# The end of an attention layer put in a written order: sums and norms on four engines, and GpSimd's weight scaling tied to VectorE

## The chip, the cores and the metric

One core of a Trainium2 chip runs the whole program in one launch. The metric is device time in microseconds (us), the median of the runs; lower is better. Five engines matter: TensorE (PE) multiplies, VectorE (DVE) and ScalarE (ACT) work on elements and read the products out of PSUM, GpSimd (POOL) works on elements in SBUF, and SyncE (SP) issues the DMA transfers. Each works through its own list of instructions in order, and semaphores tie the lists together.

## The reference

A decoder trunk for one sequence of 512 tokens of width 1024 in float32: a pooling layer, then a stick-breaking attention layer with 16 heads of 64, each followed by a squared-ReLU MLP of width 4096, all with a norm before and after. The part around the change is this:

```python
# attention layer (layer 1); k, v were projected from the stream after layer 0
h = rms_norm(x, mix_pre_g[layer])
q = jnp.matmul(h, w_q[j]).reshape(B, S, N_HEADS, HEAD_DIM).transpose(0, 2, 1, 3)
o = stick_breaking_attention(q, k, v)
m = jnp.matmul(o.transpose(0, 2, 1, 3).reshape(B, S, HD), w_o[j])
x = x + rms_norm(m, mix_post_g[layer])
h = rms_norm(x, mlp_pre_g[layer])          # then the MLP on h
...
def rms_norm(x, g):
    y = xf * lax.rsqrt(jnp.mean(xf * xf, axis=-1, keepdims=True) + EPS)
    return (y * g.astype(jnp.float32)).astype(x.dtype)
```

The gains of the norms before the k, q and v projections are applied to the rows of the weights.

## The kernel before, in words

Tokens are held in four tiles of 128 (`t` = 0 to 3), the width in eight chunks of 128. Products of full precision are made of three fast ones (`mm3`): each operand is split into a high part (a cast to fp32r, on ScalarE) and a low part (operand minus high part, on VectorE).

**Weights split ahead of their use.** Weights that are needed late are loaded, scaled if a norm's gain belongs to them, split, and stored to DRAM (`kept`) while VectorE and ScalarE have time; when they are needed, both parts are loaded from there. During attention `split_here` and `low_here` do this one tile at a time. Each tile in `going` carries a stage. A step `W` calls `split_here`, which stores tiles whose low part is made, scales, casts the high part (`nc.scalar.copy`, L211, into one of three buffers, `xn3[:, len(here) % 3]`), and loads the next tile; it then calls `fill`, which asks for the next weight. A step `w` calls `low_here` (L227, VectorE). The tiles in order are: v6 in two halves, q4, k4, q5, k5, o0, o1, q6, k6, q7, k7, o2 to o7, and the MLP's up0 to up3. The k and q tiles of this list are scaled on GpSimd (`wide_gains`, L166), v6 on ScalarE (`gains`, L157).

**The order of attention.** `ATT_ORDER` is a list written by hand, and PE, ACT, DVE and POOL follow it exactly (`tc.manual_schedule`). The letters: `J`/`Q` project keys/queries of a pair of heads, `j`/`q` read them out of PSUM (casts L1103, L1104, L1116 on ScalarE, low parts `kl` L1106 and L1118 on VectorE), `S` scores (L1145), `G` sigmoids (L1169, L1173), `X` the scan (L1178), `M` the multiplication of its result (L1270), `T` transposes (L1194) with copies on ScalarE (L1196), `A` the product with v (L1204), `a` its split (`mixed_out`, L372 and L373), `V`/`v`/`F` the value projection, its sums and its operands, `O`/`o` products of the output projection for the first pairs and their sums (`out_sum`, L1234). The digits are the pair and the head or token tile. SP is not written out; the compiler's own scheduler places its transfers.

**The end.** After the list `contract` multiplies the last four chunks (pairs 4 to 7) with their weights for tile after tile (L410 to L412), adds them to `y[t]` (L518), and runs an `Update` for each tile: squares (L376, ScalarE), the gain (L445, GpSimd for one half, VectorE for the other), the factor (`rstd`, L380 and L389), the sum into the stream `x` (L457, VectorE) with squares of it, the second factor, the norm (L474), and the transpose of the normed tile (L483) with its split into `xnh`, `xnl`. Here only PE's order is written; the scheduler orders the other engines and may also move these instructions up among those of the list. The transposes of tiles 2 and 3 follow in the MLP, between its first products (L773 to L775).

Of the kernel before, what the change touches and what calls it, by code (L numbers as in the profile page):

```python
# [10 lines left out]
F32 = mybir.dt.float32  # L11
F32R = mybir.dt.float32r
ACT = mybir.ActivationFunctionType
ALU = mybir.AluOpType
# [39 lines left out]

ATT_ORDER = [
    (w[0], int(w[1:2] or 0), int(w[2:] or 0))
    for w in """V5 W N2 v5 V0 N3 W V3 F3 v0 J0 v3 F2 W j0 w Q0 q0 F1 W w V1 V2 v1 W w v2 S0 G0 X00 M00 J1 X01 V4 M01 j1
    T00 T01 F4 v4 Q1 q1 W w V6 W v6 w
    S1 G1 X10 M10 X11 Q2 M11 q2 W w J2 A0 W j2 w a0 T10 T11
    S2 G2 X20 M20 X21 Q3 M21 q3 W w J3 A1 W j3 w a1 T20 T21  # L60
    S3 G3 X30 M30 X31 Q4 M31 q4 W w J4 A2 W j4 w a2 T30 T31
    S4 G4 X40 M40 X41 Q5 M41 q5 W w J5 A3 W j5 w a3 O00 W w O01 o00 T40 o01 T41 O02 W w O03 o02 o03
    S5 G5 X50 M50 X51 Q6 M51 q6 W w J6 A4 W j6 w a4 T50 T51
    S6 G6 X60 M60 X61 Q7 M61 q7 W w J7 A5 W j7 w a5 T60 T61
    S7 G7 X70 M70 X71 W w O10 M71 O11 W w A6 o10 a6 o11 O12 W w T70 O13 T71 o12 W A7 o13 a7""".split()
]


# [16 lines left out]
def trunk(ctx, tc, x, consts, gcol, grow, pw, wup, wdn, wq, wk, wv, wo, out):  # L85
# [35 lines left out]
    def spare_tile():  # L121
        return work.tile([P, D], F32, tag="spare", name=name("spare"))
# [38 lines left out]
    def wide_gains(lo, n):  # L161

        def scaled(raw):
            c = raw.rearrange("p (k c) -> p k c", k=n)
            g = gc[:, lo : lo + n].unsqueeze(2).broadcast_to((P, n, D // n))
            nc.gpsimd.tensor_tensor(out=c, in0=c, in1=g, op=ALU.mult)  # L166

        return scaled
# [32 lines left out]
    def split_here():  # L201
        for x in [x for x in going if x[1] == 4]:
            going.remove(x)
            keep_parts(x[0], x[3], x[2])
        for x in going:
            k, m, raw, hi, scaled = x
            if m == 1 and scaled is not None:
                scaled(raw)
            elif m == 2:
                hi = x[3] = xn3[:, len(here) % 3].bitcast(F32R)  # L210
                nc.scalar.copy(hi, raw)  # L211
            x[1] += 1
        if here:
            k, src, scaled = here.pop(0)
            n = len(here) % 4
            if n < 2:
                raw = wts.tile([P, D], F32, tag="raw", bufs=2, name=name("raw"))
            else:
                raw = spare_tile() if n == 2 else work.tile([P, D], F32, tag="grow", name=name("apart"))
            with tc.issue_after(latest["sp"].ins):  # L220
                nc.sync.dma_start(raw, src)
            going.append([k, 1, raw, None, scaled])

    def low_here():
        x = next(x for x in going if x[1] == 3)
        _, _, raw, hi, _ = x
        nc.vector.tensor_tensor(out=raw, in0=raw, in1=hi.bitcast(F32), op=ALU.subtract)  # L227
        x[1] = 4
# [146 lines left out]
    def square_sum(src, junk, st, col):  # L375
        latest["act"] = nc.scalar.activation(junk, src, ACT.Square, scale=D**-0.5, accum_out=st[:, col : col + 1])  # L376
# [9 lines left out]
    def rstd(st, col, total=None):  # L386
        total = both_sums(st, col) if total is None else total
        r = st[:, col + 3 : col + 4]
        latest["pool"] = nc.gpsimd.tensor_tensor(out=r, in0=total, in1=mhalf, op=ALU.pow)  # L389
        return r  # L390
# [31 lines left out]
    class Update:  # L422
# [24 lines left out]
        def product(self, n):  # L447
            return self.beside if n and self.cuts is not NS else self.scaled

        def add(self, between=None):  # L450
            r = rstd(self.st, 0, self.total)
            if between is not None:
                with tc.issue_after(latest["dve"].ins):
                    between()
            x = xt[self.t]
            for n, cut in enumerate(self.sums):
                latest["dve"] = nc.vector.scalar_tensor_tensor(  # L457
                    out=x[:, cut], in0=self.product(n)[:, cut], scalar=r, in1=x[:, cut], op0=ALU.mult, op1=ALU.add,
                )
                if self.final:  # L460
                    nc.sync.dma_start(out[TS[self.t], cut], x[:, cut])
                else:
                    square_sum(x[:, cut], self.xn[:, cut], self.st, 4 + n)

        def rstd(self):
            self.r = rstd(self.st, 4)
# [527 lines left out]
    with tc.tile_pool(name="att", bufs=1, reuse_waits="tile") as ap:  # L994
# [244 lines left out]
        with tc.manual_schedule(engines={on.PE, on.Activation, on.DVE, on.Pool}):  # L1239
            for what, i, a in ATT_ORDER:  # L1240
                if what == "V":
                    value_product(i)
                elif what == "v":
                    value_out(i)
                elif what == "F":
                    form(i)
                elif what == "W":
                    split_here()
                    fill()
                elif what == "w":  # L1250
                    low_here()
                elif what == "N":
                    need(i)
                elif what in "JQ":
                    project(("k" if what == "J" else "q", i))
                    fill()
                elif what == "j":
                    keys(i)
                elif what == "q":
                    queries(i)  # L1260
                elif what == "S":
                    pzs[i] = scores((qs[i], ks[i]))
                elif what == "G":
                    for a in range(2):
                        ws[i, a] = sigmoids(pzs[i], a)
                elif what == "X":
                    es[i, a] = scanned(a)
                elif what == "M":
                    w = ws[i, a]
                    latest["dve"] = nc.vector.tensor_tensor(out=w, in0=w, in1=es.pop((i, a)), op=ALU.mult)  # L1270
                elif what == "T":
                    parts[i, a] = transposed(ws.pop((i, a)))
                elif what == "A":
                    mix_pair(i)
                elif what == "a":
                    mixed_out(i)
                elif what == "O":
                    out_product(i, a)
                    if a == T - 1:
                        fill()  # L1280
                elif what == "o":
                    out_sum(i, a)
        assert not here and not going, (here, going)
        with tc.issue_after(latest["sp"].ins):
            gpost1, gpre1 = gain_row(R_MIX_POST1), gain_row(R_MLP_PRE1, spare_tile())
        wos[2] = [get(("o", 4 + c)) for c in range(4)]
        behind.update(latest)
        fill(2)
        with tc.manual_schedule(engines={on.PE}):
            contract([os[4 + c] for c in range(4)], wos[2], y, False, lambda t, y: Update(t, gpost1, y, gpre=gpre1),  # L1290
                     range(T), True)


    with tc.tile_pool(name="mlp1", bufs=1, reuse_waits="tile") as mp:
# [64 lines left out]
```

## Time and profile before

| | |
|---|---|
| time, median of 3 runs | 921.25 us (920.29 to 921.39) |
| profiled execution | 918.29 us, span 916.5 us |
| mean granted clock of TensorE | 0.991 |
| PE busy | 893.8 us, 98% |
| DVE, ACT, POOL busy | 713.4, 548.3, 107.9 us |
| DMA | 185.06 MB |
| attention's scores, pairs 0 to 7, begin at | 389 to 536 us of the span |
| output projection's end and its norms | about 558 to 604 us |

A row of the timeline gives the start and the length in us, the engine, the line, the operation, output and inputs, shape and count, and in brackets the idle time before it and what ended that. A row of the list of waits gives who waited, for whom, the sum in us, how often, and the longest. A row of stretches gives the bounds, the length, busy time and count for PE, weight loads, DVE, ACT and POOL, then the granted clock, the DMA share and GB/s. Rows of groups end in count, busy time, mean ns of one, and the idle time before with its releasers.

### The profile page before, as it was taken

What the parts mean: (1) busy time and instruction counts of PE and PEld (TensorE: products, weight loads), DVE (VectorE), ACT (ScalarE), POOL (GpSimd) and SP (SyncE); (2) the same over time, 40 slices, a digit from 0 to 9 for tenths busy, and PEclk for the clock granted to TensorE, in tenths of its full rate; (3) what the DMA queues carried; (4) which work ended last, traced back from release to release, by engine and by line L of the source; (5) the groups of instructions that cost most, each with busy time, mean ns of one, the idle gap of its engine ahead of it and who ended that gap; (6) DMA issues with size and microseconds to landing.
All of it is one profiled execution on the core that took longest, in us unless ns stands there. A gap on an engine that the chain in (4) does not pass through costs nothing.

```text
span 916.5 us, 11949 instructions
## 1 busy us (share of the span) xinstructions
PE 893.8 (98%) x4522; PEld 774.3 (84%) x4522; DVE 713.4 (78%) x718; ACT 548.3 (60%) x890; POOL 107.9 (12%) x94
## 2 busy tenths in 40 slices
PE   9999999999999999999999999799999999999996
PEld 7998888888888888878778877698888888888886
DVE  5966798987979876798885885765596875967956
ACT  6667756575996656557767862456554454454632
POOL 2100000000000023021210000302040300403103
PEclk9999999999999999999999999899999999999999
DMA  7443557287695904999778988232504233043102
GB/s 284 167 181 138 184 207 262 106 296 273 238 374 195 329 38 177 352 413 417 272 283 301 400 302 342 105 144 97 200 32 143 109 135 118 29 156 114 44 27 92
DMA packets 51247, 185.06 MB, mean 202 GB/s; under 512 B 5312, under 2 KB 5786, under 8 KB 51190
## 3 DMA queue, kind: packets, MB, share of 16 engines
q1 hardware_dynamic: 51042, 184.28, 54.5%
q8 instruction: 36, 0.59, 0.3%
q14 instruction: 21, 0.17, 0.1%
q10 hardware_dynamic: 148, 0.02, 0.0%
HBM read 138.14 MB, written 46.14 MB: 201 GB/s over the span
## 4 chain that ended last, share of the span: by engine, by line
PE 84%; DVE 6%; ACT 3%; DMA 3%; issue 2%; POOL 1%; SPq 0%; DVEq 0%; POOLq 0%; ACTq 0%
PE ps L660 27%; PE ps L773 14%; PE ps L775 14%; PE ps L774 14%; PE ps L1057 3%; PE ps L410 2%; PE ps L411 2%; PE ps L412 2%; PE ps L912 2%; PE ps L1145 1%; DVE e L1178 1%; DVE w L1270 1%; PE ps L1194 1%; PE ps L888 1%; DMA xn<-in_wdn 1%
## 5 line engine op out<-in xcount | busy, mean ns | idle before, releaser
L660 PE MATMUL ps<-w,a 128*128 128x512 f32 x1176 | 266.6, 379 | 0.3 <-DVE a L373 0.3
L773 PE MATMUL ps<-xnh,w 128*128 128x512 f32 (+1 forms) x704 | 253.8, 362 | 0.0
L774 PE MATMUL ps<-xnl,w 128*128 128x512 f32 (+1 forms) x704 | 253.6, 361 | 0.0
L775 PE MATMUL ps<-xnh,w 128*128 128x512 f32 (+1 forms) x704 | 253.6, 361 | 0.0
L660 PEld LDWEIGHTS ps<-w,a 128*128 128x128 f32 x1176 | 222.1, 189 | 32.4 <-DVE a L373 0.8
L775 PEld LDWEIGHTS ps<-xnh,w 128*128 128x128 f32 x704 | 133.7, 190 | 15.6
L774 PEld LDWEIGHTS ps<-xnl,w 128*128 128x128 f32 x704 | 133.8, 190 | 15.3
L773 PEld LDWEIGHTS ps<-xnh,w 128*128 128x128 f32 x704 | 133.3, 190 | 15.4
L148 DVE TENSOR_TENSOR w<-raw,w 128x1024 fp32r<-128x1024 f32 x56 | 70.4, 1258 | 49.7 <-ACT w L146 49.7
L146 ACT CAST w<-raw 128x1024 fp32r<-128x1024 f32 x56 | 58.5, 1045 | 78.7 <-PE ps L775 77.0
L669 DVE TENSOR_TENSOR y<-ps,y 128x512 f32<-128x512 f32 x124 | 82.6, 682 | 20.6 <-PE ps L660 20.5
L445 POOL TENSOR_TENSOR y<-y,grow 128x512 f32<-128x512 f32 x12 | 17.8, 1485 | 447.7 <-ACT xn L376 447.7
L372 ACT CAST w<-e 128x1536 fp32r<-128x1536 f32 (+1 forms) x30 | 41.8, 1392 | 44.6 <-DVE e L633 31.0
L372 ACT CAST a<-r 128x768 fp32r<-128x768 f32 (+1 forms) x60 | 47.0, 785 | 34.3 <-DVE r L614 16.6
L373 DVE TENSOR_TENSOR a<-r,a 128x768 fp32r<-128x768 f32 (+1 forms) x60 | 59.6, 994 | 3.5 <-ACT a L372 3.5
L373 DVE TENSOR_TENSOR w<-e,w 128x1536 fp32r<-128x1536 f32 (+1 forms) x30 | 54.9, 1829 | 9.4 <-ACT w L372 9.1
L1178 DVE TENSOR_TENSOR_SCAN e<-u,begin 128x1280 f32<-128x1280 f32 x16 | 48.3, 3016 | 17.7 <-ACT u L1169 16.9
L373 DVE TENSOR_TENSOR w<-xn,w 128x1536 fp32r<-128x1536 f32 (+1 forms) x20 | 33.0, 1651 | 9.5 <-ACT w L372 9.3
L373 DVE TENSOR_TENSOR w<-w,w 128x1536 fp32r<-128x1536 f32 (+1 forms) x20 | 34.5, 1727 | 6.6 <-ACT w L372 6.6
L376 ACT ACTIVATE xn<-y 128x512 f32<-128x512 f32 (+1 forms) x24 | 14.9, 619 | 40.6 <-DVE y L518 38.1
L372 ACT CAST w<-xn 128x1536 fp32r<-128x1536 f32 (+1 forms) x20 | 27.8, 1391 | 18.8 <-PE ps L660 18.8
L692 ACT ACTIVATE r<-ps 128x512 f32<-128x512 f32 x56 | 33.0, 589 | 7.9 <-PE ps L775 7.9
(172 smaller groups left out, 1315.7 us busy)
## 6 DMA issues: line engine op xcount, KB each, us to landing
w<-kept SPq DMA_DIRECT2D x82, 512.0 KB, 6.9
raw<-in_wup SPq DMA_DIRECT2D x62, 512.0 KB, 4.0
w<-in_wdn SPq DMA_DIRECT2D x8, 1536.0 KB, 6.3
xn<-in_wdn SPq DMA_DIRECT2D x8, 1536.0 KB, 6.8
kept<-xn SPq DMA_DIRECT2D x22, 512.0 KB, 5.7
kept<-apart SPq DMA_DIRECT2D x21, 512.0 KB, 6.8
kept<-wx SPq DMA_DIRECT2D x20, 512.0 KB, 4.9
kept<-raw SPq DMA_DIRECT2D x12, 512.0 KB, 7.0
```

The costliest lines, as they stand in the source:

```text
L146: nc.scalar.copy(hi, raw)
L148: nc.vector.tensor_tensor(out=lo, in0=raw, in1=hi.bitcast(F32), op=ALU.subtract)
L372: latest["act"] = nc.scalar.copy(hi, src)
L373: latest["dve"] = nc.vector.tensor_tensor(out=lo, in0=src, in1=hi.bitcast(F32), op=ALU.subtract)
L660: nc.tensor.matmul(bank, a[:, x, q, TS[t]], by_twos(w[:, z, q], NS[0]), start=start and q == 0 and k == 0, stop=q == self.n - 1 and k == 2 ...
L669: nc.vector.tensor_tensor(out=part, in0=bank, in1=part, op=ALU.add)
L692: nc.scalar.activation(split_up(r, 256), in_order(pu, 256), ACT.Relu)
L773: nc.tensor.matmul(pu[:, cols], wh[:, k, :], xh, start=k == 0, stop=False)
L774: nc.tensor.matmul(pu[:, cols], wh[:, k, :], xl, start=False, stop=False)
L775: nc.tensor.matmul(pu[:, cols], wl[:, k, :], xh, start=False, stop=k == KC - 1)
L1057: nc.tensor.matmul(bank, a[x][q], in_turn(w[q // 2][z][:, cols], 512), start=(i == 0 or not linked) and q == 0 and n == 0, stop=q == 3 and ...
L1178: nc.vector.tensor_tensor_scan(out=e[:, ::-1], data0=us[a][:, 1:][:, ::-1], data1=begin[:, ::-1], initial=0.0, op0=ALU.mult, op1=ALU.max,)
```

## The change: what it does

1. `wide_gains` first copies its eight columns of gains into a small tile on VectorE (`gain`, two buffers) and scales with that copy on GpSimd. A new step `g` (`scale_here`) does the scaling; `split_here` no longer scales. A tile is loaded at one `W`, marked at the next, scaled at the `g` after that, and cast at the following `W`, as before. `g` stands behind each `w` and some other steps of the list up to pair 4. v6's scaling on ScalarE moves to its `g` as well.
2. In the line of pair 7, `O10 o10` now stand ahead of the second scan, `a6` and the sums stand earlier, and the splits of up1, up2 and up3 stand later, among O13, T71 and A7. The two rows of gains for the norms are loaded at a new step `R` behind the store of up2.
3. The end is written out within the same manual schedule on all four engines; `contract` is no longer used for it. `Update.add` is cut into `factor` and `sums_added` so that they can stand apart. Four weights of the MLP are asked for ahead of it (before: two), and `behind`, which orders the MLP's weight splits, is noted after it.

```diff
-    for w in """... J0 v3 F2 W j0 w Q0 q0 F1 W w V1 V2 v1 W w v2 S0 G0 X00 M00 J1 X01 V4 M01 j1
-    T00 T01 F4 v4 Q1 q1 W w V6 W v6 w
...
+    for w in """... J0 v3 F2 g W j0 w g Q0 q0 F1 W w g V1 V2 v1 W w v2 S0 G0 X00 M00 J1 X01 V4 M01
+    j1 g T00 T01 F4 v4 Q1 q1 W w g V6 W v6 w g
+    S1 G1 X10 M10 X11 Q2 M11 q2 W w g J2 A0 W j2 w a0 g T10 T11
+    S2 G2 X20 M20 X21 Q3 M21 q3 W w g J3 A1 W j3 w a1 g T20 T21
+    S3 G3 X30 M30 X31 Q4 M31 q4 W w g J4 A2 W j4 w a2 g T30 T31
...
-    S7 G7 X70 M70 X71 W w O10 M71 O11 W w A6 o10 a6 o11 O12 W w T70 O13 T71 o12 W A7 o13 a7""".split()
+    S7 G7 X70 M70 O10 o10 X71 W M71 O11 A6 o11 a6 O12 T70 o12 w O13 T71 W o13 w A7 W R w W a7""".split()
...
         def scaled(raw):
             c = raw.rearrange("p (k c) -> p k c", k=n)
-            g = gc[:, lo : lo + n].unsqueeze(2).broadcast_to((P, n, D // n))
+            g = att_pool[0].tile([P, KC], F32, tag="gain", bufs=2, name=name("gain"))
+            nc.vector.tensor_copy(g, gc[:, lo : lo + n])
+            g = g.unsqueeze(2).broadcast_to((P, n, D // n))
             nc.gpsimd.tensor_tensor(out=c, in0=c, in1=g, op=ALU.mult)
...
             k, m, raw, hi, scaled = x
-            if m == 1 and scaled is not None:
-                scaled(raw)
-            elif m == 2:
+            if m == 0:
+                x[1] = 1
+            elif m == 2 or m == 1 and scaled is None:
                 hi = x[3] = xn3[:, len(here) % 3].bitcast(F32R)
                 nc.scalar.copy(hi, raw)
-            x[1] += 1
+                x[1] = 3
...
+    def scale_here():
+        for x in going:
+            if x[1] == 1 and x[4] is not None:
+                x[4](x[2])
+                x[1] = 2
...
+            product(0, 0, range(3))
+            product(0, 1, range(3))
+            product(0, 0, [3])
+            evacuate(0, 0)
+            product(0, 1, [3])
+            evacuate(0, 1)
+            ups[0].factor()
+            for t in range(1, T):
+                up, done = ups[t], ups[t - 1]
+                product(t, 0, range(4))
+                evacuate(t, 0)
+                done.sums_added()
+                if t < T - 1:
+                    product(t, 1, range(4))
+                    if t == 2:
+                        ups[0].transpose()
+                    evacuate(t, 1)
+                    done.rstd()
+                    up.factor()
+                else:
+                    product(t, 1, [0])
+                    ups[1].transpose()
+                    product(t, 1, range(1, 4))
+                    done.rstd()
+                    evacuate(t, 1)
+                    up.factor()
+                done.norm()
+            up.sums_added()
+            up.rstd()
+            up.norm()
+            pending.update({t: ups[t] for t in (T - 2, T - 1)})
         behind.update(latest)
-        fill(2)
-        with tc.manual_schedule(engines={on.PE}):
-            contract([os[4 + c] for c in range(4)], wos[2], y, False, lambda t, y: Update(t, gpost1, y, gpre=gpre1),
-                     range(T), True)
```

Here `evacuate(t, n)` adds the product to `y` on VectorE and calls `Update.square` for that half.

More of the change, by code (lines that the diff above doesn't have):

```diff
@@ L221, in split_here @@
                 nc.sync.dma_start(raw, src)
-            going.append([k, 1, raw, None, scaled])
+            going.append([k, 0, raw, None, scaled])
+    def scale_here():
[3 more added lines that the diff above has]
+                x[1] = 2
     def low_here():
@@ L448, in product, with factor, sums_added @@
             return self.beside if n and self.cuts is not NS else self.scaled
[L450 to L454, printed above, removed]
+        def factor(self):
+            self.r = rstd(self.st, 0, self.total)
+        def sums_added(self):
             x = xt[self.t]
@@ L457, in add @@
                 latest["dve"] = nc.vector.scalar_tensor_tensor(
-                    out=x[:, cut], in0=self.product(n)[:, cut], scalar=r, in1=x[:, cut], op0=ALU.mult, op1=ALU.add,
+                    out=x[:, cut], in0=self.product(n)[:, cut], scalar=self.r, in1=x[:, cut],
+                    op0=ALU.mult, op1=ALU.add,
                 )
@@ L463, in add @@
                     square_sum(x[:, cut], self.xn[:, cut], self.st, 4 + n)
+        def add(self, between=None):
+            self.factor()
+            if between is not None:
+                with tc.issue_after(latest["dve"].ins):
+                    between()
+            self.sums_added()
         def rstd(self):
@@ L1251, in trunk @@
                     low_here()
+                elif what == "g":
+                    scale_here()
+                elif what == "R":
+                    with tc.issue_after(latest["sp"].ins):
+                        gpost1, gpre1 = gain_row(R_MIX_POST1), gain_row(R_MLP_PRE1, spare_tile())
                 elif what == "N":
@@ L1282, in trunk @@
                     out_sum(i, a)
[L1283 to L1286, printed above, removed]
+            assert not here and not going, (here, going)
+            w = [get(("o", 4 + c)) for c in range(4)]
+            fill(4)
+            ups = [Update(t, gpost1, y[t], gpre=gpre1) for t in range(T)]
+            sums = {}
@@ new lines, in product, with evacuate @@
+            def product(t, n, cs):
+                if (t, n) not in sums:
+                    sums[t, n] = ps()
+                for c in cs:
+                    (lh, ll), (wh, wl) = os[4 + c], w[c]
+                    mm3(
+                        sums[t, n], lh[:, TS[t]], ll[:, TS[t]], by_twos(wh, NS[n]), by_twos(wl, NS[n]), c == 0, c == 3,
+                    )
+            def evacuate(t, n):
+                part = y[t][:, NS[n]]
+                nc.vector.tensor_tensor(out=part, in0=sums.pop((t, n)), in1=part, op=ALU.add)
+                ups[t].square(n, part, nc.vector if n else nc.gpsimd)
```

7 lines of the change are left out of this document (2 added, 5 removed).

## The prediction

> **What bounds the kernel now.** I read the page's table of engines first, then the list of waits for TensorE alone, then stretches of 2 us around those waits, then the timeline of each engine there.
>
> ```profile
> PE 893.8 (98%) x4522; PEld 774.3 (84%) x4522; DVE 713.4 (78%) x718; ACT 548.3 (60%) x890; POOL 107.9 (12%) x94
> PE ps L483 <- DVE xn L474: 5.9, 1, 5.9
> PE ps L1145 <- DVE kl L1106: 2.3, 1, 2.3
> PE ps L1194 <- DVE y L1234: 2.2, 1, 2.2
> PE ps L1145 <- ACT at L1196: 0.9, 1, 0.9
> ...
> 456.00:458.00 2.00, 2.00 (x7) 1.64 (x7) 0.79 (x1) 2.00 (x7) 0.97 (x1) 0.50 0.92 205
> 474.00:476.00 2.00, 2.00 (x17) 1.76 (x16) 1.38 (x2) 1.14 (x3) 0.00 (x0) 1.00 0.98 289
> 552.00:554.00 2.00, 2.00 (x7) 1.57 (x6) 2.00 (x4) 1.96 (x4) 0.00 (x0) 0.50 1.03 383
> ```
>
> The first row says that TensorE (PE) works 98% of the span, so almost the only time to win is where it waits, and any new wait is paid in full. The next four rows are its long waits: 5.9 us at the transposes of the output projection, 2.3 and 0.9 us at the scores of pairs 3 and 4, 2.2 us at a transpose of pair 7. The last three rows give, in the column before the DMA share, the granted TensorE clock: it is 0.50 shortly after the waits of 2.3 and 2.2 us, and 1.00 after the one of 0.9. So a wait over some 2 us is paid twice, the second time as a stretch at half clock.
>
> **Part 1: scaling tied to VectorE's order (steps `g`).** The scalings that it would part from VectorE are these:
>
> ```profile
> 440.10 1.90 POOL L166 TENSOR_TENSOR raw<-raw,gc 128x1024 f32<-128x1024 f32 x1 [23.48 <-DMA raw<-in_wq]
> ...
> 440.35 2.99 DVE L1270 TENSOR_TENSOR w<-w,e 128x1280 f32<-128x1280 f32 x1
> ...
> 529.50 1.49 DVE L1270 TENSOR_TENSOR w<-w,e 128x1280 f32<-128x1280 f32 x1
> ...
> 578.67 1.28 POOL L445 TENSOR_TENSOR y<-y,grow 128x512 f32<-128x512 f32 x1 [3.26 <-ACT xn L376]
> ...
> 578.75 0.68 DVE L518 TENSOR_TENSOR y<-ps,y 128x512 f32<-128x512 f32 x1
> ```
>
> The same multiplication takes VectorE 2.99 us beside a scaling of q6 and 1.49 alone: it waits the GpSimd instruction out. One input in PSUM, and nothing happens (0.68 under a POOL multiplication). Now GpSimd starts when it finds its tile; with `g` it starts when VectorE has passed the `w` before it, and the operations that follow there (`kl`) read PSUM. So the 1.5 us per collision are saved. But look who waits for the scaling. In ATT_ORDER stands `q3 W w g J3 A1 W j3`: the second `W` casts q6, the tile that this `g` scales, and ScalarE works in this order, with the four casts of k3 (`j3`) behind it.
>
> ```profile
> 433.77 0.82 PE L1145 MATMUL ps<-k,q 128*128 128x512 f32 x4
> 453.59 0.82 PE L1145 MATMUL ps<-k,q 128*128 128x512 f32 x4 [2.29 <-DVE kl L1106]
> 473.57 0.82 PE L1145 MATMUL ps<-k,q 128*128 128x512 f32 x4 [0.90 <-ACT at L1196]
> 518.37 0.82 PE L1145 MATMUL ps<-k,q 128*128 128x512 f32 x4
> 535.56 0.82 PE L1145 MATMUL ps<-k,q 128*128 128x512 f32 x4
> ...
> 443.59 1.05 ACT L211 CAST xn<-raw 128x1024 fp32r<-128x1024 f32 x1
> 446.62 0.58 ACT L1103 CAST k<-ps 64x512 fp32r<-64x512 f32 x1 [1.97 <-PE ps L775]
> 448.40 0.59 ACT L1104 CAST k<-ps 64x512 fp32r<-64x512 f32 x1
> ...
> 532.45 1.23 DVE L227 TENSOR_TENSOR raw<-raw,xn 128x1024 f32<-128x1024 f32 x1
> 533.70 1.39 DVE L1106 TENSOR_TENSOR kl<-ps,k 64x512 fp32r<-64x512 f32 x2
> ```
>
> The PE rows are scores S2, S3, S4, S6, S7. From S6 to S7 nobody waits: 17.19 us, TensorE's own time of a pair. In that undisturbed pair the `w` ends at 533.68, 15.31 after the scores. From S2 on this gives: 15.31, gain copy and hand-over some 0.25 (an estimate, a tenth of the `w` and two hand-overs), scaling 1.90, cast of q6 1.05, the four casts of k3 448.99-446.62=2.37, `kl` 1.39, hand-overs 0.25: S3 at 22.5 after S2. Before it was 453.59-433.77=19.82, so q6 costs +2.7: the collisions saved are overpaid, since the cast at 443.59 now runs some 8 us later and `kl` with it. S3 to S4 is the same with q7, about 0.3 longer, since the copies of transposed weights also come late on ScalarE and hold the sigmoids: 22.8 against 473.57-453.59=19.98, +2.8. The half clock: 19.98-17.19-0.90=1.89 is what followed S3's wait; it stays there, and after S4 it is new, as TensorE would be ready at 17.19+1.89=19.1 and wait 3.7: +1.9. The other scalings of this group (k6, k7) run while VectorE waits for sigmoids: 0. Sum 7.4. Bounds: +4 if `kl` starts on the first of the four casts and the clock dip is missing, +9 if both dips lengthen. I take 7.4, from the nearest rows.
>
> Earlier, q4 to k5:
>
> ```profile
> 387.64 1.06 ACT L211 CAST xn<-apart 128x1024 fp32r<-128x1024 f32 x1
> 388.76 1.22 DVE L227 TENSOR_TENSOR raw<-raw,xn 128x1024 f32<-128x1024 f32 x1
> 390.29 0.60 ACT L1169 ACTIVATE u<-ps 128x511 f32<-128x511 f32 x1 [1.59 <-PE ps L1145]
> ...
> 410.60 1.29 DVE L1073 TENSOR_TENSOR v<-ps,v 128x512 f32<-128x512 f32 x2
> 411.39 0.89 PE L1057 MATMUL ps<-w,s 128*128 128x512 f32 x3 [0.44 <-issue]
> ```
>
> The cast at 387.64 is q4's; its `g` now stands after the `w` at 388.76, which ends at 389.98. Scaled at 392.1, cast until 393.2: the first sigmoids slip from 390.29 to 393.3, and J1, which needs a bank that they free, waits some 2 us. Then k4's scaling (after `j1`) meets two SBUF additions of F4, and v4, for which V6 waits at 411.39, comes 2.1 later. The late cast of q5 costs another 0.5 before S2. Together +2.6; bounds 0 (all inside VectorE's idle time) and +4.5 (a clock dip after J1). The reordered scalings of v6 on ScalarE: 0, they lie beside V products. The gain copies, ten or so of 8 columns: 0 beside the slack of 0.43 us between `kl` (535.09) and S7 (535.56).
>
> **Part 2: last splits and sums moved (pair 7).**
>
> ```profile
> 550.87 1.42 PE L1194 MATMUL ps<-ident,w 128*128 128x128 f32 x6 [2.17 <-DVE y L1234]
> 565.02 0.48 PE L410 MATMUL ps<-h,ohl 128*128 128x512 f32 x1 [0.26 <-ACT ohl L372]
> 566.24 0.38 PE L412 MATMUL ps<-h,ohl 128*128 128x512 f32 x1
> ...
> 552.04 1.04 ACT L211 CAST xn<-raw 128x1024 fp32r<-128x1024 f32 x1 [5.92 <-DVE ohl L373]
> ...
> 547.00 0.38 SPq L199 DMA_DIRECT2D kept<-xn  x1
> ...
> DMA to landing us min/median/max: 5.0/5.2/5.3
> ```
>
> T70 waited for a bank held by O10's sum; `o10` now stands ahead of X71, so 2.17 and its half clock of 1.9 go: A7 would end 19.9 after S7, and the 18 products that need no a7 at 23.8 (before, the first that needs it ran at 565.02-535.56=29.5). What is late next is on ScalarE and SP. The high parts of up2 and up3 both go to `xn3[:, 0]`, so up3's cast must wait until up2's store has landed: that is the 5.92 us at 552.04, with the store issued at 547.00 and 5.0 to 5.3 to landing. In the new order both casts stand after T71, and a7's cast stands behind them: up2 cast by 19.4, landed 24.5, up3 cast 25.6, a7's high 26.2, VectorE's low of up3 and then of a7 27.6. The third product of the last chunk, 566.24-535.56=30.7 before, comes at 27.7: -3.0, not -4.1 with more. The DMAs moved with it (gain rows behind up2's store, up3's store behind them on SP) are needed some us later than they land: 0. Bounds: -6.9 (a7 not held, TensorE goes through at 23.8) and +1 (a store of 9 us).
>
> **Part 3: norms in a fixed order.**
>
> ```profile
> 577.46 1.04 PE L483 MATMUL ps<-ident,xn 128*128 128x128 f32 x8
> 587.60 1.97 PE L483 MATMUL ps<-ident,xn 128*128 128x128 f32 x8 [5.86 <-DVE xn L474]
> 592.62 0.49 PE L773 MATMUL ps<-xnh,w 128*128 128x256 f32 x3
> ...
> L474 DVE SCALAR_TENSOR_TENSOR xn<-x,stat,spare 128x512 f32<-128x512 f32 x8 | 7.6, 996 | 1.3 <-POOL stat L389 1.3
> L518 DVE TENSOR_TENSOR y<-ps,y 128x512 f32<-128x512 f32 x8 | 5.3, 683 | 2.9 <-PE ps L412 2.9
> L376 ACT ACTIVATE xn<-x 128x512 f32<-128x512 f32 x8 | 5.0, 628 | 6.8 <-DVE x L457 6.8
> ```
>
> From 566.6 (first half of tile 0 complete) to the next MLP's first product at 592.62 it took 26.0: the wait of 5.86, about 2.2 of half clock behind it (0.9 on the transposes, 1.97 against 1.04, and some 1.3 by estimate on the six products after them), so 17.9 of work. In the new order tile 1's norm stands on VectorE behind tile 0's two low parts, which wait for ScalarE's two high parts, which stand behind two squares of x (0.63 each); then the sum of tile 2's second half (0.68), its square, gain, factor, and the norm (0.75 a half without GpSimd beside it). Walked through with these means, the transposes of tile 1 start 20.2 after that point while TensorE is ready at 16.7 (its work so far, and the dip of part 2): a wait of 3.5 in place of 5.86. Its half clock stays (2.2), and part 2's wait of 2.4 at the last chunk brings one of its own (1.9): 17.9+1.9+3.5+2.2=25.5, and some 0.5 because tile 1's low part comes after the norms on VectorE, again 26.0. So 0; bounds -6 (chain entirely hidden) and +2. That four weights of the next MLP are asked for ahead of the projection, not two, and that `behind` is noted after it: 0, since they take tiles that the projection's own weights hold until its last chunks.
>
> **Sum.** +7.4+2.6-3.0+0=+7.0. The profiled execution took 918.29 (span 916.5), which gives 925.3; the median of the three runs, 921.25, lies 3.0 above it, so I predict 928.
>
> A page bears on the dips: the Trainium skill, "TensorE: Matmul & The Clock Gate", section "HAM oscillation — how this bites in real kernels", states that TensorE should have no idle gaps above about 3.4 us. By it gaps of 2.2 and 2.4 would be free, and the sum would be +5.1. The rows at 456 and 552 show half clock after gaps of 2.29 and 2.17, so I go by the rows.
>
> **Rivals.** (a) Faster: q6's and q7's casts are not held, because the scaling ends before J3's product is read at 446.62. Then S2 to S3 and S3 to S4 both shrink to 17.19 (-2.6, -2.8), part 1's early part is 0, part 2 stays: -8.4, 913. It decides at whether the scaling starts before 443.6; for it speaks only that ScalarE is idle there, against it that VectorE's `w` ends at 449. 0.17. (b) No change: the whole tail is won, -6.9 and -2 from the shorter gap there, and part 1 costs only its surest piece of 7.4 and 1.5: 921. 0.12. (c) Dearer: J1's gap halves the clock (+1.9), and the last store lands late (+4): 934. 0.12. (d) The gap at the last chunk stays without half clock (the rule above, in this kernel's terms): -1.9, 926. 0.05; one gap of 0.90 had none, those of 2.2 had it.
>
> **How the numbers follow.** The forecast has 0.54. Without a change a measurement here can tell about 0.2% (919.4 to 923.1). Faster: (a) and a part of (b), 0.20. Same: the rest of (b) and the low end of the forecast, 0.10. Slower: 0.70. The range 915 to 934 leaves out most of (a) and the top of (c). The forecast's own range, slower cases only, is 924 to 933.
>
> **What would show it.** S2 to S3 and S3 to S4 of 22 to 23 us with the cast of q6 starting after a POOL row near 451; no 2.99 at L1270; T70 without a wait; up3's cast idle until a landing, and a7's cast behind it; a wait of 3 to 4 at tile 1's transposes (L483). The prediction fails if the casts of k3 still start at PE's heels, or if VectorE passes `g` earlier than its list says.

## The result, and the profile after

The changed kernel takes 930.58 us (median; 930.00 to 934.45) where the kernel before takes 920.77 (920.01 to 921.39): 1.0116 times as long, 95% interval 1.0087 to 1.0145. It is slower by some 10 us. The forecast was 928, with a range of 915 to 934. The profiled executions lie 11.7 us apart: 930.0 (span 928.2) against 918.29 (span 916.5).

The list of TensorE's waits after the change (who, for whom, the sum in us, how often, the longest):

```profile
PE ps L1160 <- ACT at L1211: 7.7, 3, 4.6
PE ps L418 <- ACT ohl L380: 7.0, 1, 7.0
PE ps L498 <- DVE xn L489: 3.3, 1, 3.3
```

The numbers of the lines have moved: L1160 are the scores, L418 to L420 the three products of the output projection, L498 the norms' transposes, L788 the other weights' products. Two waits that the change was built around are smaller: the transposes wait 3.3 us instead of 5.9, and T70's 2.2 us is off the list. Above them stand two larger ones: 7.7 us at the scores (3.2 before, in the two rows shown), and 7.0 us at the last chunk of the output projection, where there had been 0.26. The timeline after, TensorE first, then the other engines that made these waits:

```profile
418.93 0.75 PE L1160 MATMUL ps<-k,q 128*128 128x512 f32 x4
437.92 0.82 PE L1160 MATMUL ps<-k,q 128*128 128x512 f32 x4 [0.63 <-ACT at L1211]
459.95 1.43 PE L1160 MATMUL ps<-k,q 128*128 128x512 f32 x4 [4.61 <-ACT at L1211]
482.84 1.08 PE L1160 MATMUL ps<-k,q 128*128 128x512 f32 x4 [2.44 <-ACT at L1211]
546.48 0.83 PE L1160 MATMUL ps<-k,q 128*128 128x512 f32 x4
578.22 0.80 PE L418 MATMUL ps<-h,ohl 128*128 128x512 f32 x1 [7.01 <-ACT ohl L380]
599.95 1.97 PE L498 MATMUL ps<-ident,xn 128*128 128x128 f32 x8 [3.32 <-DVE xn L489]
604.30 0.50 PE L788 MATMUL ps<-xnh,w 128*128 128x256 f32 x3
...
449.05 1.49 DVE L1290 TENSOR_TENSOR w<-w,e 128x1280 f32<-128x1280 f32 x1
453.15 0.16 DVE L166 COPY gain<-gc 128x8 f32<-128x8 f32 x1
453.45 1.90 POOL L168 TENSOR_TENSOR raw<-raw,gain 128x1024 f32<-128x1024 f32 x1 [28.71 <-DVE gain L166]
455.38 1.04 ACT L213 CAST xn<-raw 128x1024 fp32r<-128x1024 f32 x1 [7.57 <-POOL raw L168]
456.45 0.58 ACT L1118 CAST k<-ps 64x512 fp32r<-64x512 f32 x1
458.84 1.41 DVE L1121 TENSOR_TENSOR kl<-ps,k 64x512 fp32r<-64x512 f32 x2 [5.52 <-ACT k L1119]
...
565.34 1.07 ACT L213 CAST xn<-raw 128x1024 fp32r<-128x1024 f32 x1
567.54 0.63 SPq L201 DMA_DIRECT2D kept<-xn  x1
576.63 1.04 ACT L213 CAST xn<-raw 128x1024 fp32r<-128x1024 f32 x1 [10.22 <-issue]
577.58 0.58 ACT L380 CAST ohl<-ps 128x512 fp32r<-128x512 f32 x1
```

The first five rows are scores S1, S2, S3, S4 and S7. The middle group is one pair, read from its second row downwards as a chain: VectorE's gain copy ends at 453.31, GpSimd scales q6 from 453.45, ScalarE has idled 7.57 us for that tile and casts it at 455.38, the four casts of k3 stand behind it, `kl` behind them, and S3 begins at 459.95 after 4.61 us of idle TensorE. (What released S3 last is not `kl` but the first copy of transposed weights, L1211 at 459.31, which stands behind the same casts on ScalarE.) VectorE's multiplication (L1290) takes 1.49 here, not 2.99: the collision is gone, as the change intends. The last group is the tail: up2 is cast at 565.34, its store is issued at 567.54, up3's cast starts at 576.63, and a7's cast, for which TensorE waits, stands behind it.

Stretches of 2 us (granted TensorE clock and DMA share are the second and third number from the right, GB/s the last):

```profile
460.00:462.00 2.00, 2.00 (x8) 1.73 (x10) 1.94 (x3) 1.93 (x5) 0.00 (x0) 0.50 0.97 397
484.00:486.00 2.00, 2.00 (x10) 1.59 (x11) 1.16 (x3) 2.00 (x6) 0.73 (x1) 0.50 0.96 393
574.00:576.00 2.00, 0.00 (x0) 0.00 (x0) 0.00 (x0) 0.00 (x0) 0.00 (x0) 0.93 1.01 412
600.00:602.00 2.00, 2.00 (x9) 2.00 (x10) 2.00 (x4) 0.81 (x3) 0.01 (x1) 0.50 0.28 111
```

Half clock follows the waits of 4.61, 2.44 and 3.32 us. At 574 no compute engine does anything at all, and the 16 DMA engines are busy throughout (a share of 1.01).

The stages between the same instructions, after minus before, add up to the difference of the spans (S5 to S7, and what lies before S0 and behind the last row, differ by under 0.1):

| stage | before | after | difference | forecast |
|---|---|---|---|---|
| S0 to S2 (q4 to q5) | 44.70 | 48.87 | +4.2 | +2.6 |
| S2 to S3 (q6) | 19.82 | 22.03 | +2.2 | +2.7 |
| S3 to S4 (q7) | 19.98 | 22.89 | +2.9 | +2.8 |
| S4 to S5 (half clock) | 27.68 | 29.32 | +1.6 | +1.9 |
| S7 to the last chunk's first product (pair 7) | 29.46 | 31.74 | +2.3 | -3.0 |
| from there to the next MLP's product at L788 (norms) | 27.60 | 26.08 | -1.5 | 0 |

For pair 7 the forecast counted to the third product of the last chunk, not to the first: 30.7 before, 27.7 forecast, 33.1 measured.

### The profile page after: what moved, and what is told of

It is laid out like the page before. It is cut to its first block, busy times and chain, and to the rows that moved or that the text cites. A ratio compares the mean times of both kernels' runs of the same rounds, so it can differ in the third digit from the quotient of the medians.

```text
span 928.2 us, 11963 instructions
## 1 busy us (share of the span) xinstructions
PE 897.6 (97%) x4522; PEld 778.4 (84%) x4522; DVE 702.5 (76%) x726; ACT 548.1 (59%) x890; POOL 105.5 (11%) x94
## 4 chain that ended last, share of the span: by engine, by line
PE 84%; DMA 4%; DVE 4%; ACT 3%; issue 3%; POOL 1%; POOLq 0%; DVEq 0%; ACTq 0%
PE ps L675 26%; PE ps L788 14%; PE ps L789 14%; PE ps L790 14%; PE ps L1072 2%; PE ps L420 2%; PE ps L418 2%; PE ps L419 2%; DMA w<-kept 2%; PE ps L1160 2%; PE ps L927 2%; DMA kept<-xn 1%; PE ps L1219 1%; PE ps L903 1%; DMA xn<-in_wdn 1%
## 5 line engine op out<-in xcount | busy, mean ns | idle before, releaser
L788 PE MATMUL ps<-xnh,w 128*128 128x512 f32 (+1 forms) x704 | 255.0, 364 | 2.3 <-ACT w L1188 1.5
L788 PEld LDWEIGHTS ps<-xnh,w 128*128 128x128 f32 x704 | 133.9, 191 | 18.0 <-ACT w L1188 1.6
L789 PEld LDWEIGHTS ps<-xnl,w 128*128 128x128 f32 x704 | 134.4, 191 | 15.5
L1193 DVE TENSOR_TENSOR_SCAN e<-u,begin 128x1280 f32<-128x1280 f32 x16 | 45.2, 2823 | 17.2 <-ACT u L1184 16.5
L380 ACT CAST w<-w 128x1536 fp32r<-128x1536 f32 (+1 forms) x20 | 27.8, 1391 | 17.2 <-PE ps L675 15.9
```

Source lines behind the costliest of these rows:

```text
L380: latest["act"] = nc.scalar.copy(hi, src)
L788: nc.tensor.matmul(pu[:, cols], wh[:, k, :], xh, start=k == 0, stop=False)
L789: nc.tensor.matmul(pu[:, cols], wh[:, k, :], xl, start=False, stop=False)
L1193: nc.vector.tensor_tensor_scan(out=e[:, ::-1], data0=us[a][:, 1:][:, ::-1], data1=begin[:, ::-1], initial=0.0, op0=ALU.mult, op1=ALU.max,)
```

## The experiments

Times are medians, and ratios are to the kernel before, run in turn with each on the same chip. The beginning S0 differs by up to 3 us between profiles of these kernels, so stages are compared by differences within one profile.

**untied: the change with part 1 undone.**

```diff
-            g = att_pool[0].tile([P, KC], F32, tag="gain", bufs=2, name=name("gain"))
-            nc.vector.tensor_copy(g, gc[:, lo : lo + n])
+            g = gc[:, lo : lo + n]
...
-            if m == 0:
-                x[1] = 1
-            elif m == 2 or m == 1 and scaled is None:
+            if m == 1 and scaled is not None:
+                scaled(raw)
+            elif m == 2:
...
```

> The changed kernel with part 1 undone: the scalings are back in the steps W and free of VectorE's order; the new line of pair 7 and the written end stay. Theory (the ties cost some 10.9 us, since between the starts of S0 and S5 the changed kernel loses 10.9 us against the one before, and its end loses 0.8): about 921 to 922 us, S2 to S3 near 19.8 and S3 to S4 near 20.0. Rival (the written end costs most, and the ties save their collisions): 930 or more.

922.57 us, ratio 1.0021 (1.0006 to 1.0036). S2 to S3 takes 19.74, S3 to S4 19.95. The timeline of this kernel:

```profile
455.36 0.88 PE L1152 MATMUL ps<-k,q 128*128 128x512 f32 x4 [2.29 <-DVE kl L1113]
569.27 0.79 PE L410 MATMUL ps<-h,ohl 128*128 128x512 f32 x1 [7.23 <-ACT ohl L372]
442.20 2.91 DVE L1282 TENSOR_TENSOR w<-w,e 128x1280 f32<-128x1280 f32 x1
```

S3's wait is 2.29 again and the multiplication takes 2.91 (2.99 before), while the wait of 7 us at the last chunk stays. So part 1 makes nearly all of the loss, and the tail's wait belongs to part 2. Parts 2 and 3 together cost some 2 us: S7 to the next MLP takes 59.3 against 57.1 in this profile (57.8 in the changed kernel's), and the ratio's interval begins just above 1.

**tied_only: the kernel before with part 1 alone** (the lists up to pair 4 with `g`, pair 7 and the end as before).

```diff
-            if m == 1 and scaled is not None:
-                scaled(raw)
...
+                elif what == "g":
+                    scale_here()
```

> The kernel before with part 1 alone. Theory: slower than before by 10 to 12 us, 931 to 933, with S2 to S3 near 22.0 and S3 to S4 near 22.9. Rival (the ties cost nothing or gain): 918 to 921.

927.33 us, ratio 1.0069 (1.0046 to 1.0092), below the 931 to 933 that was expected. From S0 to S5 it takes 123.0 as the changed kernel does (123.1; before 112.2), so the +10.8 of part 1 is there in full. But S7 to the next MLP takes 52.2 us, not the 57.1 of before, with the same text of the end:

```profile
597.50 1.32 PE L491 MATMUL ps<-ident,xn 128*128 128x128 f32 x8
```

These are the transposes that waited 5.86 us in the kernel before; no wait stands at the row. Before the change the compiler orders this end on all engines but TensorE, and it ordered VectorE's norms in another way here. So the wait that part 3 attacks is no property of the algorithm, and a comparison with this end can carry some 5 us that have nothing to do with the edit.

**own_buffer: the change with a third buffer for up3's high part.**

```diff
-                hi = x[3] = xn3[:, len(here) % 3].bitcast(F32R)
+                hi = x[3] = xn3[:, 2 if k == ("up", 1, 3) else len(here) % 3].bitcast(F32R)
```

> The changed kernel; only up3's high part goes to the third buffer, so that its cast needn't wait until up2's store has landed. Theory (the 7.0 us wait before the last chunk is a7's cast held behind up3's): the wait shrinks to what o7's low weights need to land, 923 to 927 us in all. Rival (TensorE waits for the DMA queues there anyway): 930, with the wait put down to a transfer.

929.53 us, ratio 1.0094 (1.0069 to 1.0119): a miss.

```profile
567.57 0.61 ACT L380 CAST ohl<-ps 128x512 fp32r<-128x512 f32 x1
574.43 0.48 PE L419 MATMUL ps<-l,ohl 128*128 128x512 f32 x1 [2.68 <-DMA l<-kept]
577.00 0.63 ACT L384 ACTIVATE xn<-y 128x512 f32<-128x512 f32 x1 [8.83 <-DMA kept<-xn]
581.35 0.69 DVE L453 TENSOR_TENSOR y<-y,grow 128x512 f32<-128x512 f32 x1 [4.66 <-DMA grow<-in_grow]
598.71 1.78 PE L498 MATMUL ps<-ident,xn 128*128 128x128 f32 x8 [4.19 <-DVE xn L489]
```

The mechanism holds: a7's cast runs at 567.57 instead of 577.58. The changed kernel's row of 576.63 names only "issue" ahead of up3's cast; with a buffer of its own the cast does not wait, so what held it was up2's store out of the buffer that it takes. But the time does not follow. TensorE waits 2.68 us for the low part of the last weights (`l`), ScalarE's squares wait for a store (the third buffer is also where the squares put their unneeded output), and VectorE waits 4.66 us for a row of gains. The norms, which follow those two, are late for TensorE's transposes twice, by 2.17 and 4.19 us. So TensorE's waits in this stretch, 7.01 and 3.32 in the changed kernel, became 2.68, 2.17 and 4.19: 9.0 us instead of 10.3.

**dve_cast: the change with q6's and q7's high parts cast by VectorE, behind `kl`.**

```diff
-                nc.scalar.copy(hi, raw)
+                if k not in (("q", 6), ("q", 7)): nc.scalar.copy(hi, raw)
... in low_here:
+        if k in (("q", 6), ("q", 7)): nc.vector.tensor_copy(hi, raw)
```

> The changed kernel; the high parts of q6 and q7 are cast by VectorE just ahead of their low parts, not by ScalarE, so that the casts of k3 and k4 are not held behind a scaling. Scalings, gain copies and their order stay. Theory (the cost of the ties in pairs 2 to 4 is ScalarE held): S2 to S3 near 17.2, S3 to S4 17.2 to 18.5, no half clock after them, 919 to 922 us. Rival (the cost is in the scaling's own place on GpSimd and VectorE): S3 and S4 as late as in the changed kernel, 930.

919.49 us, ratio 0.9993 (0.9978 to 1.0008): 11.1 us under the changed kernel with two casts moved.

```profile
454.87 1.41 DVE L1124 TENSOR_TENSOR kl<-ps,k 64x512 fp32r<-64x512 f32 x2
456.61 0.83 PE L1163 MATMUL ps<-k,q 128*128 128x512 f32 x4
456.90 0.69 DVE L237 CAST xn<-raw 128x1024 fp32r<-128x1024 f32 x1 [0.63 <-POOL raw L168]
460.24 4.13 DVE L1196 TENSOR_TENSOR_SCAN e<-u,begin 128x1280 f32<-128x1280 f32 x1 [0.58 <-ACT u L1187]
474.91 0.82 PE L1163 MATMUL ps<-k,q 128*128 128x512 f32 x4 [0.86 <-DVE kl L1124]
```

`kl` now stands ahead of the cast, S3 does not wait, and S2 to S3 takes 17.18, the length of an undisturbed pair. From S2 to S5 it is 63.2 us (74.2 in the changed kernel, 67.5 before). So the loss in the middle was the place of the cast on ScalarE and not the scaling. Against the kernel before it is 4.3 us shorter: S3's wait of 2.29 and the half clock behind it are gone. S4's wait is not (0.86, before 0.90): the scan ahead of it takes 4.13 us beside the scaling of k6 (459.79 to 461.69), where the next one takes 2.83, a collision that the tie doesn't avoid.

Whether the tie or the moved cast wins the 4.3 is not shown, since no run moves the casts without the tie. For the tie speaks that both multiplications ahead of S3 take 1.49 here and took 2.99 and 2.90 before, and that in the kernel before ScalarE stood idle for 1.97 us ahead of k3's casts, so that the cast of q6 held nothing there.

**late_ties: dve_cast with the ties of v6, q4, k4, q5 and k5 undone.**

```diff
...
             if m == 0:
                 x[1] = 1
+                if scaled is not None and not hasattr(scaled, "tied"):
+                    scaled(raw)
+                    x[1] = 2
...
```

> The kernel dve_cast with the ties of v6, q4, k4, q5 and k5 undone as well (scaled in their W again, as before the change); only q6 to k7 stay tied, with q6 and q7 cast by VectorE. Theory (holding q4's and q5's casts cost 3.7 us before S2): S0 to S1 near 27.6, S1 to S2 near 17.2, 915 to 917 us. Rival (S1 and S2 came late for another reason): 919 to 920 as dve_cast.

917.33 us, ratio 0.9952 (0.9933 to 0.9972): faster than before, and just above the 915 to 917 that was expected. S0 to S2 takes 45.3 (48.5 in dve_cast, 48.9 in the changed kernel), S0 to S5 108.5 (before 112.2). So the early ties cost 3 us or a little more and gained nothing. What is left is the tail, S7 to the next MLP in 58.4 us.

**splits_early: the change with the third buffer, the splits of up2 and up3 back where they stood, and step R behind them.**

```diff
-    S7 G7 X70 M70 O10 o10 X71 W M71 O11 A6 o11 a6 O12 T70 o12 w O13 T71 W o13 w A7 W R w W a7
+    S7 G7 X70 M70 O10 o10 X71 W w M71 O11 W w A6 o11 a6 O12 W w R T70 O13 T71 o12 W A7 o13 a7
...
```

> The changed kernel with up2's and up3's splits back where the old line of pair 7 had them, up3's high part in the third buffer, and the gain rows asked for after them; O10's sum stays ahead of the second scan. Theory (a7 is late because of the splits in front of it, and the stores and loads bunched there hold o7 and the gain rows): the last chunk starts some 24 to 26 us after S7, not 31.7, no wait for a gain row, 922 to 925 us. Rival (the DMA queues are full there whatever the order): a wait for a transfer of 3 us or more remains, 928 or more.

931.71 us, ratio 1.0097 (1.0074 to 1.0121): the theory falls, the rival holds.

```profile
563.66 0.58 PE L418 MATMUL ps<-w,ohl 128*128 128x512 f32 x1 [2.50 <-DVE y L1249]
580.09 0.48 PE L419 MATMUL ps<-l,ohl 128*128 128x512 f32 x1 [4.05 <-DMA l<-kept]
570.10 0.46 SPq L329 DMA_DIRECT2D l<-kept  x1
```

The last weights' low part, issued at 570.10, is used at 580.09, ten microseconds later, and O13 now waits 2.50 us for VectorE, on which low parts of the splits stand ahead of `o11`.

**low_later: the change with tile 0's transposes and splits behind tile 1's norm.**

```diff
                     product(t, 1, range(4))
-                    if t == 2:
-                        ups[0].transpose()
                     evacuate(t, 1)
...
                 done.norm()
+                if t == 2:
+                    ups[0].transpose()
```

> The changed kernel; only tile 0's split (two casts, two low parts) stands behind tile 1's norm on ScalarE and VectorE; TensorE's order stays. Theory (tile 1's norm is late because it stands behind tile 0's low parts): the wait of 3.3 us at tile 1's transposes falls to 1.3 or less and its half clock goes, 926 to 928 us. Rival (VectorE's sum of work sets that time): the wait stays near 3, 930.

932.36 us, ratio 1.0102 (1.0069 to 1.0135), the same as the changed kernel's.

```profile
602.99 1.32 PE L498 MATMUL ps<-ident,xn 128*128 128x128 f32 x8 [0.79 <-DVE xn L489]
```

The transposes wait 0.79 instead of 3.32, no half clock follows, and from the last chunk to the next MLP it takes 24.0 instead of 26.1. So the reason for that wait, tile 0's low parts ahead of tile 1's norm on VectorE, is shown. The expected 926 to 928 is missed all the same. Part of the gain comes back as a new wait, 1.80 us at the first MLP product for ScalarE's high part, which now comes later. And the time can't tell the rest: the last chunk's own wait was 8.13 in this profile, against 7.01, S0 to S5 took 124.8 with the same instructions that took 123.1, and S7 to the next MLP is 1.0 shorter, which is inside the interval.

**combined: late_ties, splits_early and low_later together.**

> The three edits together: late_ties, splits_early and low_later. If they add: -14, -7 and -3 from the changed kernel, 905 to 909 us, faster than the kernel before by 1.3% or more. Rival (each only uncovers the next wait): 914 or more.

916.47 us, ratio 0.9936 (0.9913 to 0.9959): faster than before, but 7 to 11 us above what the parts would give if they added, as the rival has it. Its longest wait is for the low part of the last weights, the next (2.5) O13's for VectorE, both as in splits_early:

```profile
PE ps L430 <- DMA l<-kept: 4.5, 1, 4.5
```

**loads_later and own_loads: the four MLP weights asked for behind tile 0's sums**, on combined and on late_ties with the third buffer.

```diff
             w = [get(("o", 4 + c)) for c in range(4)]
-            fill(4)
...
             ups[0].factor()
+            fill(4)
```

> combined, with the four MLP weights that are asked for ahead of the output projection's end (fill(4)) asked for behind tile 0's sums instead. Theory (the low part of o7 lands late because three loads of MLP weights and two of raw rows share the 16 queues with it): it lands some 4 us earlier, the wait of 4.5 us for it falls to under 1.5 us, and the time to 912 to 914, unless the first MLP product then waits for its weights. Rival (it is late for the stores and gain rows ahead of it): the wait stays at 3.5 us or more and the time at 916 to 917.

> late_ties with up3's high part in the third buffer (as in own_buffer) and with the same four MLP weights asked for behind tile 0's sums. Here no group of products stands behind the splits of up2 and up3, so O13's wait of 2.5 us isn't there. Theory (both the buffer and the queue were the cause): the wait of some 7 us ahead of the last chunk falls to under 1 us and the wait for the gain row in tile 0's sum to under 2 us: 917.3 - 6 + 1 to 3 for what is uncovered behind, 912 to 914. Rival (the stores fill the queue): the wait for l or for the gain row stays at 2.7 us and more, 915 to 917.

loads_later: 916.09 us, ratio 0.9948 (0.9927 to 0.9968), and the wait for `l` is 4.1 us: the rival holds. The transfers that I had taken for MLP weights are the projection's own (four weights, each in a high and a low part); the loads that the edit concerns are issued at 559.2 and 584.3, and in combined they were at 557.3 and 583.5, so they were not ahead of `l` (554.46 there) in the first place. own_loads: 915.14 us, ratio 0.9943 (0.9923 to 0.9962), again the rival's side: `l` is waited for 2.52 us, and the row of gains, issued at 555.77, is what VectorE waits for. Its timeline:

```profile
567.93 0.69 DVE L464 TENSOR_TENSOR y<-y,grow 128x512 f32<-128x512 f32 x1 [5.04 <-DMA grow<-in_grow]
555.77 0.44 SPq L126 DMA_DIRECT2D grow<-in_grow  x1
```

**end_before: the kernel before with part 1 as in late_ties, and the old end.**

> The kernel before with part 1 as in late_ties (the ties kept for q6, k6, q7, k7 alone, the high parts of q6 and q7 cast by VectorE), and with the old end. It tells what parts 2 and 3 are worth. Scores of pair 0 to scores of pair 5 should take 108.5 us as in late_ties. Theory A (the old end as the kernel before has it, S7 to the first MLP product 57.1 us): late_ties' end takes 58.4 us, so this comes out 1.3 us below late_ties, 916. Theory B (the norms of the end in the order that tied_only got, 52.2 us): 6.2 us below late_ties, 911. Theory C (parts 2 and 3 are worth something that the span from S7 to the first MLP product doesn't show): above late_ties, 919 or more.

915.48 us, ratio 0.9941 (0.9919 to 0.9962). S0 to S5 takes 108.5 and S7 to the next MLP 57.3: theory A, the compiler's old end, of whose waits the two longest are:

```profile
PE ps L502 <- DVE xn L493: 4.0, 1, 4.0
PE ps L430 <- DMA l<-kept: 2.7, 1, 2.7
```

Its interval overlaps with late_ties' (0.9933 to 0.9972): parts 2 and 3 as they stand in late_ties win nothing that can be measured.

**rows_first: own_loads with the rows of gains asked for ahead of the last two splits.**

```diff
-    ... O13 T71 W o13 w A7 W R w W a7
+    ... O13 T71 R W o13 w A7 W w W a7
```

> own_loads with the step R (the two gain rows) ahead of the last two splits in the list, not between them. In own_loads the gain row was issued at 555.77, behind the stores of up1 and up2, and VectorE waited 5.04 us for it until 567.93. Theory (the row is late because stores stand ahead of it in full queues): issued some 1.5 to 3 us earlier it lands by 565, VectorE's wait falls to 2 us or less, the transposes' waits of 2.91 and 2.50 fall together to 3 us or less, and the time to 911 to 913. Rival (something else, such as the last chunk's products or tile 1's norm, is next): the wait for the row falls but the transposes still wait 5 us, and the time stays at 914 to 916.

913.58 us, ratio 0.9919 (0.9903 to 0.9936): the fastest of all, 7 us under the kernel before. But it is only half the theory:

```profile
552.92 0.44 SPq L126 DMA_DIRECT2D grow<-in_grow  x1
566.15 0.63 ACT L395 ACTIVATE xn<-y 128x512 f32<-128x512 f32 x1 [12.22 <-DMA kept<-xn]
567.52 1.26 DVE L464 TENSOR_TENSOR y<-y,grow 128x512 f32<-128x512 f32 x1 [5.27 <-ACT xn L395]
574.82 1.29 PE L509 MATMUL ps<-ident,xn 128*128 128x128 f32 x8 [1.89 <-DVE xn L500]
583.55 1.78 PE L509 MATMUL ps<-ident,xn 128*128 128x128 f32 x8 [4.19 <-DVE xn L500]
```

The row is no longer what ends VectorE's wait; the wait of 5 us is still there, now for ScalarE's squares, which wait for a store. The transposes wait 6.1 us together (5.4 in own_loads), so the rival describes the place better. The time lies below its 914 all the same, and the intervals of the two kernels overlap; S7 to the next MLP is 1.1 shorter (55.6 against 56.8). The clock may have a share in that: it is 1.00 behind the gap of 1.89, and 0.50 for some 3 us behind the 2.91 that own_loads has there. How much is the chip's scatter stays open.

## Why the prediction came out right

**Part 1, the middle: right in place, cause and size.** The chain was worked out from the pair between S6 and S7: S3 at 22.5 after S2 and S4 at 22.8 after S3. Measured were 22.03 and 22.89, and 1.6 us of half clock behind S4 where 1.9 stood, +6.8 in all against 7.4. The term that was a little off is the half us of S2 to S3, where the chain ran to the end of `kl`; what released S3 last was the copy of transposed weights, which the forecast had only for S4. Between S3 and S4 the split was another than forecast (half clock took some 3.3 us, by difference from 17.19, and the wait 2.44, where 1.9 and 3.7 stood), but ScalarE's and VectorE's chain set the sum. untied, tied_only and dve_cast show the cause: the cast of q6 waits for the scaling, and the casts of k3 wait behind it in ScalarE's order. Rival (a), casts not held, fails at its own condition, a scaling that starts before 443.6, which is 9.8 us after S2 in the kernel before: it starts 15.5 after S2 (453.45).

**Part 1, early: right in place, mis-sized.** The term of +2.6 measured +4.2. S0 to S1 came out at +2.3, near the 2.1 that was left for it, but of other pieces: J1 waits 1.49 us instead of some 2, and half clock follows, which the forecast had only in its upper bound. The piece that was too small is "the late cast of q5 costs another 0.5 before S2": S1 to S2 cost +1.9. These rows of the changed kernel show what stood there:

```profile
394.24 0.48 PE L788 MATMUL ps<-xnh,w 128*128 128x512 f32 x1 [1.49 <-ACT w L1188]
420.31 1.05 ACT L213 CAST xn<-raw 128x1024 fp32r<-128x1024 f32 x1 [4.12 <-POOL raw L168]
422.03 0.48 PE L788 MATMUL ps<-xnh,w 128*128 128x512 f32 x1 [0.79 <-ACT v L1090]
```

The forecast saw J1 wait, but not that q5's late cast delays v6's copies behind it on ScalarE, for a bank of which the next projection waits 0.79, and then the copies ahead of S2 for another 0.63. The remaining 0.45 of the +1.9 is not split up further.

Here is a stretch of the changed kernel behind J1's gap, then the same place in own_buffer, which runs the same list there:

```profile
396.00:398.00 2.00, 2.00 (x6) 1.63 (x5) 2.00 (x1) 2.00 (x7) 0.00 (x0) 0.50 1.02 420
...
396.10 0.48 PE L788 MATMUL ps<-xnh,w 128*128 128x512 f32 x1 [1.49 <-ACT w L1188]
396.00:398.00 2.00, 1.91 (x9) 1.69 (x10) 2.00 (x4) 2.00 (x8) 0.00 (x0) 1.00 1.03 420
```

In own_buffer the gap is the same and no half clock follows; splits_early is like it. These two take 47.2 and 47.5 us from S0 to S2, +2.5 and +2.8 against the kernel before, which is the forecast's 2.6, and the wait of 0.79 is missing in them too. The kernels with the same early list and half clock at J1 (the changed kernel, tied_only, dve_cast, low_later) take 48.5 to 50.2. So most of this term's miss goes with half clock, which came in some executions and not in others; how it leads to the wait between S1 and S2 is open. The value lies inside the bounds of 0 and +4.5. late_ties shows that these ties are the cause of the loss before S2.

**Part 2: right in mechanism, wrong in sign.** T70's wait is gone, TensorE is ready for the last chunk 24.7 us after S7 (578.22 less 7.01, less 546.48; forecast 23.8), up2's cast ends 19.9 after it (forecast 19.4), and up3's cast waits for up2's store with a7's cast behind it. What failed is the step "up2 cast by 19.4, landed 24.5": the store was issued 1.1 us after the cast and took 9.1 us until up3's cast could start, 10.2 from cast to cast where 5.1 stood. So the wait was 7.0 where the forecast had 2.4, and -3.0 became +2.3, past the bound of "+1 (a store of 9 us)" that I had named myself. I had priced the store by three stores of the kernel before between 536 and 566 us (5.0 to 5.3), while this one is one of ten transfers of 512 KB issued between 564.2 and 569.5, with the DMA share at 1.01 behind them. The step "the DMAs moved with it: 0" holds in the changed kernel as far as the rows of gains go, since GpSimd's and VectorE's first uses of one (582.35 and 583.18) wait for ScalarE. But own_buffer and rows_first show the rows and the stores as the next thing waited for. That is also why the gap of 7.0 us was not worth as much as it looks: removed, it uncovers `l`, the rows and the squares.

**Part 3: right in place, better by 1.5.** A wait of 3.5 at tile 1's transposes was forecast and 3.32 came, for the reason that was named, as low_later shows. The stage came out at -1.5 instead of 0, inside -6 and +2. Counted from the forecast's own point, the end of the third product (580.39), TensorE was ready after 16.2 us (forecast 16.7) and waited 3.3 (3.5); what was mis-sized is the rest, 4.4 us to the MLP where 5.8 stood. No wait for tile 1's low part came, for which 0.5 had been set down. tied_only adds what the forecast could not see: the 5.86 that part 3 removes was one outcome of the compiler's order.

**The sum.** +4.2+6.8+2.3-1.5=+11.7 by stages (with a rounding), against +7.0. The early miss (+1.6) and part 2's (+5.3) are partly taken back by part 3 (-1.5) and the middle (-0.6). In the medians 9.8 of the 11.7 show, since the profiled execution lay 2.5 below its median before and 0.6 after. So 928 against 930.58 is nearer than the terms are, and that is luck: errors of both signs met, and of the 3.0 us that the forecast added from profile to median only 0.6 came. The direction and the place of the largest loss were forecast for the right reason; the sign of part 2 was not. Rival (c), dearer, had two pieces, half clock behind J1's gap and a late last store, and both came, at +1.6 and +5.3 even larger together than its +5.9. Its 934 was not reached because part 3 and the middle took 2.1 back and the step from profile to median another 2.4.

**The half clock.** The rows at 484 and 600 show half clock after gaps of 2.44 and 3.32 us, as the forecast had it. Rival (d), a gap at the last chunk without half clock, was not put to the test: that gap was 7.01 us and not 2.4, and the clock behind it (576 to 580) is 0.50. The Trainium skill, "TensorE: Matmul & The Clock Gate", section "HAM oscillation — how this bites in real kernels", states that TensorE should have no idle gaps above about 3.4 us; these rows disagree with it as a bound, since gaps below it are followed by half clock. But the forecast's own rule, half clock after a gap of some 2 us, is not exact either: in own_buffer the transposes start at 589.99 after a gap of 2.17 us, and the stretch behind is at full clock.

```profile
590.00:592.00 2.00, 1.97 (x13) 1.65 (x14) 2.00 (x4) 0.86 (x3) 0.06 (x1) 1.00 0.00 0
```

## What to carry to other kernels

When an instruction is made to wait for another engine, look at its own engine's list first: what stands behind it pays for the wait, and the repair may be to move that one instruction (dve_cast: two casts moved to another engine, 11 us under the changed kernel) rather than to drop the tie. Price a store that guards a buffer by what will be queued with it after the change, not by how long such a store took before. Where the DMA engines are busy throughout, taking away one wait for DMA uncovers the next; count what is queued before hoping for the whole gap.

## What the runs showed of the hardware that I had not expected

Transfers of 512 KB took about twice as long where ten of them were issued close together. Up2's store took 9.1 us from its issue until its buffer was free, and the low part of the last weights 10 to 11 us in splits_early and combined, while the three stores shown of the kernel before landed after 5.0 to 5.3 us. At the 412 GB/s of the row at 574, one such transfer is 1.27 us of all 16 engines, so ten of them issued within 5.3 us leave some 7 us of backlog (an estimate from these numbers). The warning stood on the page of the kernel before: its list of transfers gives medians of 5.7 us for `kept<-xn`, 6.8 for `kept<-apart` and 7.0 for `kept<-raw`, all of 512 KB, so 5.0 to 5.3 was a low price.

The clock is not set by the length of one gap alone. Between 370 and 640 us of the fourteen profiles, half clock came with every TensorE gap of 2.29 us and more. Of the sixteen gaps between 1.48 and 2.17 it came with ten and not with the other six. The same gap at the same place came out both ways: 1.49 at J1 (half clock in the changed kernel, full in own_buffer), 1.80 at the first MLP product (half in combined, full in low_later), and 2.16 at T70 (half in tied_only, full in end_before). What decides is open; no run was made for it. In this kernel a gap of some 2 us therefore has to be reckoned with as one that may cost half clock, and a single profile doesn't tell.
